# A two-layer hybrid network on one core: places and number of buffers for split weights, products per bank, and the plan of the modulation blocks

## The chip, the cores and the metric

The kernel runs on one core of a Trainium2 chip. The metric is the time of one execution on the device in microseconds (us), the median of several runs. Five engines work side by side: TensorE (PE: matmuls, PEld: its weight loads), VectorE (DVE), ScalarE (ACT), GpSimd (POOL) and SyncE (SP), which here issues most of the DMAs. In the rows, "L114" is line 114 of the kernel, and times are counted from the start of the span.

## The reference, cut to what matters

One sequence of 256 tokens with 1024 features goes through two layers of three sub-layers each: an FFN, a mixer, an FFN. The mixer of the first layer is a hybrid of a gated linear recurrence and a state-space part, that of the second an mLSTM. Before each sub-layer the input is normalised and modulated by a shift and a scale, behind it a gate is applied; shift, scale and gate come from a vector `c` through a large matrix `ada_w`.

```python
c_act = jax.nn.silu(c)
for layer in range(DEPTH):
    mod = (c_act @ ada_w[layer] + ada_b[layer]).reshape(bsz, N_SUB, 3, D_MODEL)[:, :, :, None, :]

    def modulate(t, sub):
        return rms_norm(t, norm_g[layer, sub]) * (1.0 + mod[:, sub, 1]) + mod[:, sub, 0]

    h = modulate(x, 0)
    x = x + HALF_STEP * (1.0 + mod[:, 0, 2]) * swiglu(h, ffn_w_gate[layer, 0], ffn_w_up[layer, 0], ffn_w_down[layer, 0])
    h = modulate(x, 1)
    if layer % 2 == 0:
        y = hybrid_mixer(h, ...)
    else:
        y = mlstm_block(h, ...)
    x = x + (1.0 + mod[:, 1, 2]) * y.astype(x.dtype)
    h = modulate(x, 2)
    x = x + HALF_STEP * (1.0 + mod[:, 2, 2]) * swiglu(h, ffn_w_gate[layer, 1], ffn_w_up[layer, 1], ffn_w_down[layer, 1])
return rms_norm(x, final_norm_g)

def swiglu(h, w_gate, w_up, w_down):
    return (jax.nn.silu(h @ w_gate) * (h @ w_up)) @ w_down
```

All of it is in float32; the FFN's inner width is 2816, that is 22 blocks of 128.

## The kernel before, in words

**Layout.** Activations are kept transposed, features on the partitions and the 256 tokens along the free dimension: `x` is eight tiles of 128 x 256. The six sub-layers s = 0 to 5 are FFN, hybrid, FFN, FFN, mLSTM, FFN; "the third FFN" is s = 3.

**Weights.** All weights are one stream of 2928 tiles of 128 x 128, in the order of use, cut into 366 pieces of eight tiles (128 x 1024 float32, 512 KB each). `Weights._piece` (L97) loads a piece into a raw buffer (L101, on SP's queue; pool `rawp`, three buffers), ACT rounds it to a high part `whi` (L113), and VectorE subtracts that from the raw piece and leaves the low part `wlo` (L114). Both parts live in pool `partp`, with six buffers of each. Pieces are made four ahead of use (`LEAD`). So the DMA of a piece waits for the split of the piece that had its raw buffer before, and a cast waits for a pair of parts that TensorE is done with.

**Products.** An activation is split in the same manner into a high and a low part that stand side by side (`hb` for the normalised input, `ph`, `yb`, `ysb`, `ylb` for the inputs of output projections; the split is L339 on ACT and L340 on VectorE). A product with a weight tile is the sum of three matmuls: high weight by high and by low activation, and low weight by high activation (`multiply`, L346 to L348, 256 columns each). The output projections of the FFNs and of the mLSTM make the first two with one matmul of 512 columns (L451) over both parts, into the two halves of a bank, and the third with one of 256 (L453) into the first half; VectorE then adds both halves to `x`, in two instructions (L458). The last column group of the last FFN and the hybrid's projection have three products of 256 columns.

**Places.** `PLACES` gives each piece the place of its two parts modulo 512 bytes in a partition, by an offset in a buffer that is 128 elements longer than a piece. The parts of projections stand at 448 and at 0 or 256 in turn; the second FFN's gate/up takes four sorts in turn; elsewhere two sorts in turn, with (128, 0) at every eleventh piece.

**FFN.** `ffn` (L473) starts with four banks of the first blocks on an input that isn't normalised yet (`begin`, L380, with L393 to L395), while VectorE computes the norm and then eight chunks of the normalised input: L360 on VectorE, L362 on ACT for the high part, L363 on VectorE for the low part. Then gate/up runs block by block: 16 tiles into one bank, Silu on ACT (L481), the product on VectorE (`fg`, L482), and its split (`ph`, L339 and L340). The output projection (`out_project`, L411) goes over eight column groups, each with 22 products, one for each `ph`.

**Modulation.** `ADA_PLAN` spreads the 144 blocks of `ada_w` over the pieces: for each entry a sub-layer, a range of pieces counted from its start, and the blocks. `ada_block` (L225) loads 512 KB (L230, SP's queue) and multiplies and sums on VectorE (L232). A block is issued behind the newest split. Blocks 72 to 95 are the modulation of s = 3, 96 to 119 that of s = 4. In the third FFN VectorE also prepares the mLSTM's gate weights (`mlstm_weights`, L824, with DMAs on POOL's queue).

The order of the instructions on each engine is made when the kernel is built, by a scheduler that follows priorities in program order, the dependencies, and what `behind` and `issue_after` demand.

## Time and profile before

| | us |
|---|---|
| time, median of 3 runs | 1138.89 (1138.03 to 1142.32) |
| the profiled execution, its own time | 1137.13 |
| its span | 1135.4 |
| TensorE busy | 1109.3 (98%) |
| TensorE's weight loads busy | 1057.5 (93%) |
| VectorE busy | 955.4 (84%) |
| ScalarE busy | 642.0 (57%) |
| mean granted clock of TensorE | 0.995 |
| read from HBM | 269.77 MB, mean 239 GB/s |

Busy time of an engine is the time in which at least one of its instructions was running. Matmuls are pipelined, so a matmul's own duration is longer than the step from one to the next; the step is what counts on TensorE. In rows of the timeline the bracket gives the idle time ahead of an instruction and what ended it. In the chain of waits the program is followed back from its last instruction, at each step to what released it. The profile's page cuts the span into 40 equal slices of 28.4 us; a digit is tenths.

### The profile page before, as it was taken

To read this page: it belongs to the slowest core of one execution; us is meant where nothing else is said; L and a number is where in the kernel's file an instruction comes from. 1 tells how busy PE (TensorE), PEld (TensorE's weight loads), DVE (VectorE), ACT (ScalarE), POOL (GpSimd) and SP (SyncE) were. 2 spreads that over 40 slices of the span, in tenths; PEclk is the share of its full clock that TensorE was granted. 3 is DMA by queue.
4 is the path that set the end of the run, shared out by engine and by line. 5 is a ranking of instruction groups with operands and counts; after the bars stand their busy time and mean duration, and the time that the engine had idled before them with its cause. 6 is when DMAs were issued, how large, how long until landed. Compare 5 with 4: busy or idle time off the path is not lost.

```text
span 1135.4 us, 21905 instructions
## 1 busy us (share of the span) xinstructions
PE 1109.3 (98%) x8548; PEld 1057.5 (93%) x8548; DVE 955.4 (84%) x1831; ACT 642.0 (57%) x1074; POOL 8.8 (1%) x25
## 2 busy tenths in 40 slices
PE   7999999999999999999999997999999999999997
PEld 6999988999989999998899997889999889999987
DVE  7999999999889798889889888889879988766562
ACT  4464545888976564444554444447765556554542
POOL 0000000000000000000000000010000000000000
PEclk9999999999999999999999998999999999999999
DMA  8989999555555558888849889972532374775551
GB/s 318 357 304 350 383 330 326 207 192 194 186 174 178 201 200 324 311 306 317 291 157 324 309 318 328 328 275 94 168 112 93 113 235 156 269 241 194 188 201 39
DMA packets 75273, 272.25 MB, mean 240 GB/s; under 512 B 8449, under 2 KB 9121, under 8 KB 75170
## 3 DMA queue, kind: packets, MB, share of 16 engines
q1 hardware_dynamic: 74160, 268.99, 67.4%
q8 instruction: 67, 1.10, 0.4%
q0 software_dynamic: 432, 1.10, 0.4%
q10 hardware_dynamic: 578, 0.76, 0.2%
q14 instruction: 36, 0.29, 0.1%
HBM read 269.77 MB, written 1.05 MB: 239 GB/s over the span
## 4 chain that ended last, share of the span: by engine, by line
PE 61%; DVE 18%; DMA 13%; ACT 5%; issue 3%; ACTq 0%; SPq 0%; DVEq 0%
PE od L451 12%; DMA wraw<-in_wst_dram 11%; DVE wlo L114 7%; PE gu L346 7%; PE gu L347 7%; PE gu L348 7%; PE od L453 6%; DVE ada L232 3%; ACT whi L113 3%; DVE hb L363 1%; DMA wgr<-in_ml_wg_dram 1%; DVE ht L360 1%; PE od L346 1%; PE up L347 1%; PE up L348 1%
## 5 line engine op out<-in xcount | busy, mean ns | idle before, releaser
L113 ACT CAST whi<-wraw 128x1024 fp32r<-128x1024 f32 x364 | 380.0, 1048 | 281.6 <-DMA wraw<-in_wst_dram 172.9
L114 DVE TENSOR_TENSOR wlo<-wraw,whi 128x1024 fp32r<-128x1024 f32 x366 | 446.1, 1221 | 97.1 <-ACT whi L113 95.1
L347 PE MATMUL gu<-hb,whi 128*128 128x256 f32 x1312 | 362.7, 278 | 0.1
L348 PE MATMUL gu<-hb,wlo 128*128 128x256 f32 x1312 | 362.4, 277 | 0.0
L346 PE MATMUL gu<-hb,whi 128*128 128x256 f32 x1312 | 359.1, 278 | 1.6 <-ACT hb L362 1.5
L347 PEld LDWEIGHTS gu<-hb,whi 128*128 128x128 f32 x1312 | 247.5, 189 | 0.3 <-DVE hb L363 0.3
L348 PEld LDWEIGHTS gu<-hb,wlo 128*128 128x128 f32 x1312 | 247.5, 189 | 0.0
L346 PEld LDWEIGHTS gu<-hb,whi 128*128 128x128 f32 x1312 | 245.2, 189 | 2.1 <-ACT hb L362 2.0
L451 PE MATMUL od<-ph,whi 128*128 128x512 f32 x682 | 236.2, 394 | 5.8 <-DVE ph L340 5.8
L453 PE MATMUL od<-ph,wlo 128*128 128x256 f32 x682 | 190.0, 279 | 0.0
L232 DVE SCALAR_TENSOR_TENSOR ada<-ada,cact 128x1024 f32<-128x1024 f32 x144 | 174.9, 1217 | 0.2 <-DMA ada<-in_adaT_dram 0.2
L451 PEld LDWEIGHTS od<-ph,whi 128*128 128x128 f32 x682 | 129.5, 190 | 33.7 <-DVE ph L340 6.6
L453 PEld LDWEIGHTS od<-ph,wlo 128*128 128x128 f32 x682 | 129.6, 190 | 0.0
L339 ACT CAST ph<-fg 128x256 fp32r<-128x256 f32 x88 | 35.2, 406 | 98.1 <-DVE fg L482 97.8
L458 DVE SCALAR_TENSOR_TENSOR x<-od,gate,x 128x256 f32<-128x256 f32 x87 | 41.5, 480 | 20.1 <-PE od L348 9.7
L340 DVE TENSOR_TENSOR ph<-fg,ph 128x256 fp32r<-128x256 f32 x88 | 36.6, 420 | 12.9 <-ACT ph L339 12.9
L451 PE MATMUL od<-yb,whi 128*128 128x512 f32 x128 | 44.2, 392 | 0.0
L346 PE MATMUL zz<-hb,whi 128*128 128x256 f32 x128 | 37.2, 290 | 0.0
L348 PE MATMUL zz<-hb,wlo 128*128 128x256 f32 x128 | 36.9, 288 | 0.0
L347 PE MATMUL zz<-hb,whi 128*128 128x256 f32 x128 | 36.7, 287 | 0.0
L453 PE MATMUL od<-yb,wlo 128*128 128x256 f32 x128 | 35.5, 279 | 0.0
L362 ACT ACTIVATE hb<-ht,shift 128x256 fp32r<-128x256 f32 x48 | 22.6, 505 | 22.9 <-DVE ht L360 22.9
(407 smaller groups left out, 1896.1 us busy)
## 6 DMA issues: line engine op xcount, KB each, us to landing
wraw<-in_wst_dram SPq DMA_DIRECT2D x366, 512.0 KB, 4.4
ada<-in_adaT_dram SPq DMA_DIRECT2D x144, 512.0 KB, 5.3
xn<-in_x_dram SPq DMA_DIRECT2D x2, 512.0 KB, 4.1
wgr<-in_ml_wg_dram POOLq DMA_DIRECT2D x3, 256.0 KB, 5.2
out_dram<-res ACTq DMA_DIRECT2D x2, 128.0 KB, 2.3
out_dram<-res SPq DMA_DIRECT2D x2, 128.0 KB, 2.1
out_dram<-res SPq DMA_DIRECT2D x1, 256.0 KB, 2.5
out_dram<-res ACTq DMA_DIRECT2D x1, 256.0 KB, 2.6
```

The lines of the kernel that those rows point to most:

```text
L113: raw_hi = nc.scalar.copy(hi, raw)
L114: self.last = nc.vector.tensor_tensor(out=lo, in0=raw, in1=hi.bitcast(F32), op=ALU.subtract)
L232: nc.vector.scalar_tensor_tensor(out=raw, in0=raw, scalar=1.0, in1=cact, op0=ALU.mult, op1=ALU.mult, accum_out=mods[s][:, m:m + 1])
L339: nc.scalar.copy(hi, src)
L340: nc.vector.tensor_tensor(out=both[:, 1, :], in0=src, in1=hi.bitcast(F32), op=ALU.subtract)
L346: m = nc.tensor.matmul(dst, wh, both[:, 0, :], start=start, stop=False, skip_group_check=True)
L347: nc.tensor.matmul(dst, wh, both[:, 1, :], start=False, stop=False, skip_group_check=True)
L348: nc.tensor.matmul(dst, wl, both[:, 0, :], start=False, stop=stop, skip_group_check=True)
L362: hi = nc.scalar.activation(h[k][:, 0, :], t, AF.Identity, bias=sh[:, k:k + 1])
L451: nc.tensor.matmul(bank, wh, both.rearrange("p i t -> p (i t)"), start=(k == 0), stop=False, skip_group_check=True)
L453: nc.tensor.matmul(sums[0], wl, both[:, 0, :], start=False, stop=(k == len(rhs) - 1), skip_group_check=True)
L458: nc.vector.scalar_tensor_tensor(out=xs_t[d], in0=part, scalar=g[:, d:d + 1], in1=xs_t[d], op0=ALU.mult, op1=ALU.add)
```

## The change

The parts of a piece get places by tag, in place of offsets: three tags a, b and c in turn (piece number modulo 3) with two buffers each, laid out with pads so that high and low part stand at (448, 320), (64, 448) and (448, 64) modulo 512. There are still six of each, now without the 128 spare elements. The raw ring has four buffers. The eight blocks 96 to 103 move from the plan of the third FFN to that of the second. All output projections use `project`, three matmuls of 256 columns into one half of a bank, and one addition to `x` per column group.

```diff
-PLACES = []
...
-    if _w:
-        PLACES.append((128, 192) if _w[0] in (1, 8) else (448, 256 * (_i % 2)))
-    elif _s == 2:
-        PLACES.append(((448, 320), (64, 448), (448, 64), (320, 192))[_i % 4])
-    else:
-        PLACES.append((128, 0) if _n % 11 == 6 else (448, 64 + 256 * (_i % 2)))
+PLACES = (("wloa", 320), ("whia", 448), ("whic", 448), ("wlob", 448), ("whib", 64), ("wloc", 64))
+FIRST_PLACE = 64
...
-    (2, (6, 60), range(64, 96)), (3, (6, 60), range(96, 136)), (5, (6, 40), range(136, 144)),
+    (2, (6, 60), range(64, 104)), (3, (6, 60), range(104, 136)), (5, (6, 40), range(136, 144)),
...
-        oh, ol = ((n - 64) % 512 // 4 for n in PLACES[i])
-        hi = self.part_pool.tile([P, w + 128], F32R, tag="whi", name=f"whi{i}")[:, oh:oh + w]
-        lo = self.part_pool.tile([P, w + 128], F32R, tag="wlo", name=f"wlo{i}")[:, ol:ol + w]
+        hi, lo = (self.part_pool.tile([P, w], F32R, tag=f"{n}{'abc'[i % 3]}", name=f"{n}{i}") for n in ("whi", "wlo"))
...
-    rawp = ctx.enter_context(tc.tile_pool(name="rawp", bufs=3))
-    partp = ctx.enter_context(tc.tile_pool(name="partp", bufs=6))
+    rawp = ctx.enter_context(tc.tile_pool(name="rawp", bufs=4))
+    partp = ctx.enter_context(tc.tile_pool(name="partp", bufs=2))
+    at = FIRST_PLACE
+    for tag, place in PLACES:
+        if (place - at) % 512:
+            partp.tile([P, (place - at) % 512 // 4], F32, name=f"pad_{tag}", bufs=1)
+        partp.tile([P, PIECE * P], F32R, tag=tag, name=f"place_{tag}")
+        at = place
...
-                sums = [dst]
-            elif s == 5 and d == ND - 1:
-
-                sums = [mm_bank(f"od{s}_{d}")[:, 0:T]]
-                project(sums[0], rhs)
             else:
-
-
-                bank = mm_bank(f"od{s}_{d}")
-                sums = [bank[:, 0:T], bank[:, T:2 * T]]
-                for k, both in enumerate(rhs):
-                    wh, wl = W.next()
-                    nc.tensor.matmul(bank, wh, both.rearrange("p i t -> p (i t)"), start=(k == 0), stop=False,
-                                     skip_group_check=True)
-                    nc.tensor.matmul(sums[0], wl, both[:, 0, :], start=False, stop=(k == len(rhs) - 1),
-                                     skip_group_check=True)
+                dst = mm_bank(f"od{s}_{d}")[:, 0:T]
+                project(dst, rhs)
...
-            for part in sums[::-1]:
-                nc.vector.scalar_tensor_tensor(out=xs_t[d], in0=part, scalar=g[:, d:d + 1], in1=xs_t[d],
-                                               op0=ALU.mult, op1=ALU.add)
+            nc.vector.scalar_tensor_tensor(out=xs_t[d], in0=dst, scalar=g[:, d:d + 1], in1=xs_t[d],
+                                           op0=ALU.mult, op1=ALU.add)
```

The changed kernel is shorter, so its line numbers are lower: L457 is what L482 was, L329 what L340 was, L97 what L114 was, L221 what L232 was, L433 what L458 was, L349, L352 and L395 what L360, L363 and L406 were, and L335 to L337 what L346 to L348 were. On TensorE 810 matmuls come in, on VectorE 39 instructions go.

The first place is VectorE at the end of the third FFN's gate/up, before: `ph3_20` and `ph3_21` are the last two split blocks, `wlo` the low parts of pieces, `ada` modulation blocks.

```order
L482 TENSOR_TENSOR fg3_20_8784<-fg3_20_8784,gu3_20_8720 128x256
L232 SCALAR_TENSOR_TENSOR ada124_8830,mod5_8653<-ada124_8830,cact_107 128x1024
L340 TENSOR_TENSOR ph3_20_8787<-fg3_20_8784,ph3_20_8787 128x256
L114 TENSOR_TENSOR wlo234_8868<-wraw234_8865,whi234_8867 128x1024
L114 TENSOR_TENSOR wlo235_8890<-wraw235_8887,whi235_8889 128x1024
L482 TENSOR_TENSOR fg3_21_8857<-fg3_21_8857,gu3_21_8790 128x256
L232 SCALAR_TENSOR_TENSOR ada125_8893,mod5_8653<-ada125_8893,cact_107 128x1024
L340 TENSOR_TENSOR ph3_21_8860<-fg3_21_8857,ph3_21_8860 128x256
```

The same place after:

```order
L457 TENSOR_TENSOR fg3_20_9138<-fg3_20_9138,gu3_20_9074 128x256
L221 SCALAR_TENSOR_TENSOR ada126_9181,mod5_8827<-ada126_9181,cact_116 128x1024
L329 TENSOR_TENSOR ph3_20_9141<-fg3_20_9138,ph3_20_9141 128x256
L97 TENSOR_TENSOR wlo234_9219<-wraw234_9216,whi234_9218 128x1024
L221 SCALAR_TENSOR_TENSOR ada127_9222,mod5_8827<-ada127_9222,cact_116 128x1024
L97 TENSOR_TENSOR wlo235_9252<-wraw235_9249,whi235_9251 128x1024
L457 TENSOR_TENSOR fg3_21_9208<-fg3_21_9208,gu3_21_9144 128x256
L329 TENSOR_TENSOR ph3_21_9211<-fg3_21_9208,ph3_21_9211 128x256
```

Two modulation blocks stand between `fg3_20` and `ph3_21` in both, but the second has moved ahead of `wlo235` and doesn't stand directly ahead of `ph3_21` any more. They are `ada126` and `ada127` where `ada124` and `ada125` stood; since the plan starts at block 104 and not at 96, 24 blocks of it are ahead of `ph3_21`, where 30 were.

The second place is VectorE at the end of the second FFN's gate/up, before:

```order
L114 TENSOR_TENSOR wlo168_6612<-wraw168_6609,whi168_6611 128x1024
L232 SCALAR_TENSOR_TENSOR ada87_6615,mod3_5727<-ada87_6615,cact_107 128x1024
L370 CAST hb_96<-shift3_6683 128x8x2
L259 TENSOR_TENSOR scale3_6684<-mod3_5727,cols_95 128x8
L371 TENSOR_TENSOR hb_96<-shift3_6683,hb_96 128x8x2
L260 SCALAR_TENSOR_TENSOR scale3_6684<-scale3_6684,cols_95 128x8
L114 TENSOR_TENSOR wlo169_6637<-wraw169_6634,whi169_6636 128x1024
L482 TENSOR_TENSOR fg2_21_6601<-fg2_21_6601,gu2_21_6537 128x256
L340 TENSOR_TENSOR ph2_21_6604<-fg2_21_6601,ph2_21_6604 128x256
```

And after:

```order
L97 TENSOR_TENSOR wlo168_6807<-wraw168_6804,whi168_6806 128x1024
L97 TENSOR_TENSOR wlo169_6837<-wraw169_6834,whi169_6836 128x1024
L457 TENSOR_TENSOR fg2_21_6796<-fg2_21_6796,gu2_21_6729 128x256
L221 SCALAR_TENSOR_TENSOR ada93_6840,mod3_5807<-ada93_6840,cact_116 128x1024
L329 TENSOR_TENSOR ph2_21_6799<-fg2_21_6796,ph2_21_6799 128x256
```

Here the last block of modulation ahead of `ph2_21` is `ada93`, where it was `ada87`, so 30 blocks of this plan are ahead of it, where 24 were; the shift and scale of the next sub-layer (`shift3`, `scale3`), which stood between, come earlier in the program.

The third place is VectorE and TensorE at the start of the third FFN, while the chunks of the normalised input are made (`ht3_k` is chunk k before its shift, `hb` the normalised input's parts; `gu3_f0` to `gu3_f3` are the four first banks, `gu3_2` and `gu3_3` the next blocks). VectorE before:

```order
L406 TENSOR_TENSOR fg3_0_7382<-gu3_f0_7226,rs3_7201 128x256
L363 SCALAR_TENSOR_TENSOR hb_96<-ht3_4_7366,shift3_6683,hb_96 128x256
L363 SCALAR_TENSOR_TENSOR hb_96<-ht3_5_7370,shift3_6683,hb_96 128x256
L360 SCALAR_TENSOR_TENSOR ht3_6_7374<-x_94,scale3_6684,rs3_7201 128x256
L360 SCALAR_TENSOR_TENSOR ht3_7_7378<-x_94,scale3_6684,rs3_7201 128x256
L114 TENSOR_TENSOR wlo193_7323<-wraw193_7320,whi193_7322 128x1024
L363 SCALAR_TENSOR_TENSOR hb_96<-ht3_6_7374,shift3_6683,hb_96 128x256
L363 SCALAR_TENSOR_TENSOR hb_96<-ht3_7_7378,shift3_6683,hb_96 128x256
L408 COPY shc_g3_0_7384<-gu3_f0_7226 128x1
L406 TENSOR_TENSOR fu3_0_7386<-gu3_f1_7227,rs3_7201 128x256
```

VectorE after:

```order
L97 TENSOR_TENSOR wlo194_7782<-wraw194_7779,whi194_7781 128x1024
L352 SCALAR_TENSOR_TENSOR hb_105<-ht3_4_7736,shift3_6899,hb_105 128x256
L352 SCALAR_TENSOR_TENSOR hb_105<-ht3_5_7740,shift3_6899,hb_105 128x256
L349 SCALAR_TENSOR_TENSOR ht3_6_7744<-x_103,scale3_6900,rs3_7571 128x256
L97 TENSOR_TENSOR wlo193_7693<-wraw193_7690,whi193_7692 128x1024
L352 SCALAR_TENSOR_TENSOR hb_105<-ht3_6_7744,shift3_6899,hb_105 128x256
L349 SCALAR_TENSOR_TENSOR ht3_7_7748<-x_103,scale3_6900,rs3_7571 128x256
L395 TENSOR_TENSOR fu3_0_7756<-gu3_f1_7597,rs3_7571 128x256
L397 COPY shc_u3_0_7758<-gu3_f1_7597 128x1
L395 TENSOR_TENSOR fg3_1_7760<-gu3_f2_7598,rs3_7571 128x256
L352 SCALAR_TENSOR_TENSOR hb_105<-ht3_7_7748,shift3_6899,hb_105 128x256
```

A split (`wlo194`), the products `fu3_0` and `fg3_1` and two copies now stand ahead of the last low part of `hb`. TensorE, at the products of block 2 with the last chunk (the last rows of `whi190` here), before:

```order
L347 MATMUL gu3_2_7408<-hb_96,whi190_7232 128x256
L348 MATMUL gu3_2_7408<-hb_96,wlo190_7233 128x256
L346 MATMUL gu3_2_7408<-hb_96,whi190_7232 128x256
L347 MATMUL gu3_2_7408<-hb_96,whi190_7232 128x256
L348 MATMUL gu3_2_7408<-hb_96,wlo190_7233 128x256
L346 MATMUL gu3_2_7408<-hb_96,whi191_7262 128x256
```

And after:

```order
L336 MATMUL gu3_3_7845<-hb_105,whi192_7662 128x256
L337 MATMUL gu3_3_7845<-hb_105,wlo192_7663 128x256
L335 MATMUL gu3_2_7778<-hb_105,whi190_7602 128x256
L335 MATMUL gu3_3_7845<-hb_105,whi192_7662 128x256
L336 MATMUL gu3_3_7845<-hb_105,whi192_7662 128x256
L337 MATMUL gu3_3_7845<-hb_105,wlo192_7663 128x256
L335 MATMUL gu3_3_7845<-hb_105,whi192_7662 128x256
L336 MATMUL gu3_3_7845<-hb_105,whi192_7662 128x256
L336 MATMUL gu3_2_7778<-hb_105,whi190_7602 128x256
L337 MATMUL gu3_2_7778<-hb_105,wlo190_7603 128x256
L335 MATMUL gu3_2_7778<-hb_105,whi191_7632 128x256
```

In the order after, matmuls of block 3 (`gu3_3`) stand between those of block 2; eleven of them are ahead of the row that reads the last chunk's low part (the second L336 of `gu3_2`).

## Rows read from the trace of the kernel before

**Rows 1.** The page: busy time of each engine over the span (us, share, instructions), and the granted clock of TensorE in 40 slices.

```profile
PE 1109.3 (98%) x8548; PEld 1057.5 (93%) x8548; DVE 955.4 (84%) x1831; ACT 642.0 (57%) x1074; POOL 8.8 (1%) x25
...
PEclk9999999999999999999999998999999999999999
```

**Rows 2.** The page: the chain of waits that ended last, share of the span by engine.

```profile
PE 61%; DVE 18%; DMA 13%; ACT 5%; issue 3%; ACTq 0%; SPq 0%; DVEq 0%
```

**Rows 3.** Busy time by stage: start and end of each stretch in us, its length, each engine's busy us and its instructions, TensorE's granted clock, share of the DMA engines, GB/s. The stretches are the first FFN's gate/up from 60 us on, the second FFN's gate/up and output projection, the third's gate/up and output projection.

```profile
60.00:139.00 79.00, 79.00 (x696) 79.00 (x696) 73.41 (x120) 42.47 (x68) 0.00 (x0) 1.00 0.95 351
...
402.30:512.00 109.70, 109.54 (x962) 109.12 (x961) 92.38 (x143) 58.03 (x87) 0.00 (x0) 1.00 0.82 294
512.00:572.40 60.40, 60.40 (x359) 53.51 (x358) 51.64 (x82) 30.61 (x41) 1.06 (x2) 1.00 0.87 296
584.80:694.10 109.30, 109.30 (x962) 109.30 (x961) 95.69 (x159) 52.31 (x79) 1.08 (x2) 1.00 0.85 300
694.10:764.30 70.20, 64.44 (x358) 56.20 (x357) 60.02 (x91) 33.17 (x47) 2.67 (x7) 0.93 0.87 313
```

**Rows 4.** TensorE's timeline in the third FFN's output projection: start in us, duration in us, engine, line, operation, tiles, shapes, and in brackets the idle time before it and what ended it.

```profile
700.66 0.39 PE L451 MATMUL od<-ph,whi 128*128 128x512 f32 x1
700.88 0.28 PE L453 MATMUL od<-ph,wlo 128*128 128x256 f32 x1
703.82 0.79 PE L451 MATMUL od<-ph,whi 128*128 128x512 f32 x1 [2.66 <-DVE ph L340]
...
707.93 0.79 PE L451 MATMUL od<-ph,whi 128*128 128x512 f32 x1 [3.10 <-DVE ph L340]
...
708.73 0.63 PE L451 MATMUL od<-ph,whi 128*128 128x512 f32 x1
...
709.37 0.63 PE L451 MATMUL od<-ph,whi 128*128 128x512 f32 x1
...
713.85 0.48 PE L451 MATMUL od<-ph,whi 128*128 128x512 f32 x1
```

**Rows 5.** VectorE's timeline in the same stretch.

```profile
703.35 0.42 DVE L340 TENSOR_TENSOR ph<-fg,ph 128x256 fp32r<-128x256 f32 x1
703.70 2.36 DVE L114 TENSOR_TENSOR wlo<-wraw,whi 128x1024 fp32r<-128x1024 f32 x2
...
706.31 1.22 DVE L232 SCALAR_TENSOR_TENSOR ada<-ada,cact 128x1024 f32<-128x1024 f32 x1
...
707.46 0.42 DVE L340 TENSOR_TENSOR ph<-fg,ph 128x256 fp32r<-128x256 f32 x1
```

**Rows 6.** Waits in the third FFN's gate/up, 584.8 to 694.1 us: who waited for what, us in total, times, longest us.

```profile
ACT whi L113 <- DMA wraw<-in_wst_dram: 26.3, 19, 3.1
```

**Rows 7.** Waits of SP's queue over the whole span, same columns.

```profile
SPq L101 <- DVE wlo L114: 554.8, 243, 16.5
```

**Rows 8.** The page: DMA issues, with count, KB each and median us from issue to landing.

```profile
wraw<-in_wst_dram SPq DMA_DIRECT2D x366, 512.0 KB, 4.4
```

**Rows 9.** VectorE's timeline: the split of the last `ph` of the first FFN and of the second.

```profile
142.69 0.42 DVE L340 TENSOR_TENSOR ph<-fg,ph 128x256 fp32r<-128x256 f32 x1
...
518.53 0.43 DVE L340 TENSOR_TENSOR ph<-fg,ph 128x256 fp32r<-128x256 f32 x1 [0.47 <-ACT ph L339]
```

**Rows 10.** TensorE's timeline at the ends of stretches without a wait: two wide pairs of the first FFN's projection, three pieces of the hybrid's projection, three pieces of the second FFN's gate/up, one piece of the third's.

```profile
149.89 0.39 PE L451 MATMUL od<-ph,whi 128*128 128x512 f32 x1
...
150.23 0.39 PE L451 MATMUL od<-ph,whi 128*128 128x512 f32 x1
...
352.90 0.28 PE L346 MATMUL od<-ysb,whi 128*128 128x256 f32 x1
...
361.46 0.28 PE L346 MATMUL od<-ysb,whi 128*128 128x256 f32 x1
...
452.20 0.28 PE L346 MATMUL gu<-hb,whi 128*128 128x256 f32 x1
...
460.36 0.28 PE L346 MATMUL gu<-hb,whi 128*128 128x256 f32 x1
...
620.35 0.28 PE L346 MATMUL gu<-hb,whi 128*128 128x256 f32 x1
...
623.18 0.28 PE L346 MATMUL gu<-hb,whi 128*128 128x256 f32 x1
```

**Rows 11.** The timeline of ACT, then of TensorE, in the hybrid's output projection.

```profile
368.12 1.05 ACT L113 CAST whi<-wraw 128x1024 fp32r<-128x1024 f32 x1 [1.06 <-DMA wraw<-in_wst_dram]
...
366.81 0.38 PE L346 MATMUL od<-ylb,whi 128*128 128x256 f32 x1 [0.55 <-ACT ylb L339]
...
369.53 0.51 PE L346 MATMUL od<-ylb,whi 128*128 128x256 f32 x2 [0.72 <-ACT ylb L339]
```

**Rows 12.** VectorE's timeline at the start of the third FFN.

```profile
585.12 1.22 DVE L114 TENSOR_TENSOR wlo<-wraw,whi 128x1024 fp32r<-128x1024 f32 x1
586.26 0.87 DVE L363 SCALAR_TENSOR_TENSOR hb<-ht,shift,hb 128x256 fp32r<-128x256 f32 x2
...
587.12 0.41 DVE L406 TENSOR_TENSOR fu<-gu_f,rs 128x256 f32<-128x256 f32 x1
587.45 0.14 DVE L408 COPY shc_u<-gu_f 128x1 f32<-128x1 f32 x1
```

**Rows 13.** The page: the group of the additions to `x` behind output projections: count, busy us, mean ns of one, idle time before and its releaser.

```profile
L458 DVE SCALAR_TENSOR_TENSOR x<-od,gate,x 128x256 f32<-128x256 f32 x87 | 41.5, 480 | 20.1 <-PE od L348 9.7
```

9 lines of the change are left out of this document (removed).

## Prediction, made before the change was run

> **What bounds the kernel now.** I began with the page's busy row and the row of granted clock: TensorE is busy for 1109.3 of 1135.4 us, VectorE for 955.4, and one of the 40 slices, the 26th, has a lower clock [rows 1]. The chain's groups come next: TensorE has 61% of the chain, but VectorE has 18% and DMA 13%, so in places the weights' supply ends last [rows 2]. To find the place I cut the span by stage [rows 3]. The FFNs' gate/up stretches are full of matmuls: 109.54 of 109.70 us in the second FFN, 109.30 of 109.30 in the third. The output projections differ: 60.40 us in the second FFN, all busy at clock 1.00; 70.20 us in the third, with 64.44 busy at 0.93. Same instructions, 9.8 us more. The timeline of TensorE in that stretch shows why [rows 4]: after 700.88 it waits 2.66 us, after one more pair 3.10 us, both for `ph` of L340 on VectorE, and then runs at the lower of its two levels (1.2 GHz): pairs every 0.64 us (708.73, 709.37) until about 713.85, where the same pair takes 0.34 in a warm stretch [rows 10]. From 700.66 to 713.85 there are 11 pairs: 13.19 us against 11 x 0.34 = 3.74, so the stall costs 9.45 us.
>
> VectorE's rows say what was late [rows 5]. Gate/up ended at 694.10, yet block 20's `ph` starts at 703.35 and block 21's at 707.46, and ahead of each stands a split (L114) and a modulation block (L232). VectorE wasn't full: 95.69 of 109.30 us busy, 13.6 us idle [rows 3], while ACT's casts waited 26.3 us in this stretch for a raw piece to land [rows 6]. The issue of a raw piece in turn waits for the split three pieces earlier, 554.8 us over the run on SP's queue [rows 7], and a transfer takes 4.4 us at the median [rows 8], against the 2.72 us in which TensorE uses one up (452.20 to 460.36 is three pieces) [rows 10]. So third-FFN VectorE falls behind for two reasons together: it has 40 modulation blocks, and a late piece can't be made good, since the raw ring is only three deep.
>
> **The change part by part.** The sum is made against the profiled execution, 1137.1 us (span 1135.4); it is 1.8 us under the median of 1138.9.
>
> *Modulation moved, with the fourth raw buffer: -9.4 us.* The last `ph` is the 22nd factor of the projection's first column group, so TensorE comes to it 21 pairs after 694.10, at 694.10 + 21 x 0.34 = 701.2; it ended at 707.46 + 0.42 = 707.9, which is 6.7 us late [rows 5]. By the two orders, 30 modulation blocks (96 to 125) stand ahead of it before and 24 (104 to 127) after. Each takes VectorE 1.15 us from its start to the start of the next instruction (706.31 to 707.46) [rows 5], so six fewer give 6.9 us: alone this would just do. The fourth buffer adds one piece, 2.72 us, of lead to each transfer, and fewer DMAs of 512 KB compete there, so the 26.3 us of late pieces shrink too. I take all 9.45 us; bounds 0 (stall as before) and -9.8 (both projections equal).
>
> Those six stand ahead of the second FFN's last `ph` now, 6.9 us, and all eight cost VectorE 9.2 there. It is busy 92.38 of 109.70 us in gate/up: 17.3 us of cover, and 8.8 more in the projection [rows 3]. But the slack at the end is small now: the last `ph` ends at 518.53 + 0.43 = 518.96 [rows 9], and TensorE comes to it at 512.0 + 21 x 0.34 = 519.1. So the second FFN is on time only if its idle time, which is waiting for late pieces, really shrinks. For that speaks the first FFN: with 24 blocks on 26 pieces, a higher rate than 40 on 54, its last `ph` ends at 143.11 [rows 9] where 139.0 + 7.14 = 146.1 would do, and TensorE stays full with three buffers, at 351 GB/s [rows 3]. The second FFN of the change wants 54 weight pieces and 40 blocks, 94 x 0.524 MB, in 54 x 2.72 = 147 us: 335 GB/s, below this. I take 0; bounds 0 and +9.4 (the stall moves here whole).
>
> *Three products in one bank: 0.* Per tile two matmuls (512 and 256 columns) become three of 256. The wide pair goes 149.89 to 150.23, 0.340 us; three narrow ones take (460.36 - 452.20)/72 = 0.1133 each, 0.340 together [rows 10]. 810 tiles change (682 + 128), and the columns are the same 768. The step from two bank halves to one drops 39 evacuations (L458) of 0.480 us, 18.7 us of VectorE [rows 13]; nearly all lie beside matmuls, so I count 0 on the path. Bounds: -2 (a few stand ahead of the next norm) and, where the slow step below holds, +13.6.
> The Trainium skill ("TensorE: Matmul & The Clock Gate", section "Back-to-back issue gap") gives the isolated gap of a warm matmul as N/2.4 + 2.5 ns, so that a third matmul pays the fixed part once more: 810 x 2.5 ns = an estimate of 2.0 us slower. The rows above show 0.340 us both ways, so here the trace doesn't agree; by the page the time would come out at 1128.
>
> *Places: -4.0 us.* Before, the sort (128, 0), at every eleventh narrow piece outside the second FFN, is slow: such a piece runs from 620.35 to 623.18, 2.83 us in place of 2.72 [rows 10]. There are 20 of them: 20 x 0.11 = 2.2 us. In the hybrid's projection the step is 118.9 ns: 352.90 to 361.46 is three pieces, 8.56/72 [rows 10]. The second FFN's gate/up, where sorts already take turns, runs at 113.3 (452.20 to 460.36); the change uses three of its four sorts everywhere, so I expect 113.3 elsewhere too. The hybrid's projection has 16 pieces; two fall on the waits below, and 14 x 24 x 5.6 ns = 1.9 us, of which I take 1.8; bounds -6 (all stretches above 113.3) and the slow step's cost as a rival below.
>
> *Fourth raw buffer elsewhere: -1.3 us.* In the hybrid's projection ACT waits 1.06 us for a raw piece, and its `ylb` cast, queued behind that whi cast, holds TensorE 0.55 and 0.72 us [rows 11]; 2.72 us more of lead covers both. Bounds 0 and -2.5 (the same again in slower matmuls behind the waits).
>
> *The other side: norms, +1.7 us.* The change's VectorE order at the start of the third FFN has a split (wlo194) and two L395 (the old L406) ahead of the last chunk's low part which before came behind it. Their steps are 1.14 (585.12 to 586.26) and 0.33 (587.12 to 587.45): 1.14 + 2 x 0.33 = 1.8 us [rows 12]. TensorE's order has eleven matmuls moved ahead of the first that reads this chunk: 11 x 0.113 = 1.25. Before, no wait and no spare is shown; so I take 0.55 us of waiting, in the last three sub-layers, whose orders are alike: 1.7. Bounds 0 and +5.4 (each loses the 1.8).
>
> SP and POOL issue the same DMAs in the same number; only the eight move, each behind an earlier split. The splits read and write as many bytes as before. 0 for both.
>
> Sum: -9.4 - 4.0 - 1.3 + 1.7 = -13.0, so 1124.1 in a profiled run; 1.8 more for the median: **1126 us**.
>
> **The rivals.** *The stall moves to the second FFN.* Then 9.4 us come back: 1126 + 9.4 = 1135. For it: a slack of 0.1 us against 6.9 us more work ahead; the second FFN then carries what the third did before, but for the third's preparation of mLSTM gate weights. Against it: 17.3 us idle, the fourth buffer, the first FFN's rows. 0.15.
> *Stall stays in the third FFN*, if six blocks fewer don't do and the fourth buffer gives no lead (because the next DMA still queues behind other transfers), also about 1135. Against it: 6.9 us freed for 6.7 late. 0.06.
> *The slow step holds (slower).* 118.9 against 113.3 ns is 16.8 ns a tile. It shows in a projection with three products, the hybrid's, and there it lasts for three pieces in a row; the wide pairs don't have it [rows 10]. If three products in the 810 changed tiles run at it: +13.6 us, 1140, no gain left; it decides from 13.0/0.0168 = 774 tiles. Gate/up has 352 tiles in each of four FFNs; with half of these 1408 too, 11.8 us more: 1151, the price I give this rival. Against it: 72 matmuls in a row at 113.3 with these sorts. 0.08.
>
> **How the numbers follow.** Forecast 0.64, rivals 0.15, 0.06, 0.08; 0.07 is left for effects I name no price for, on both sides. A measurement tells 0.5% from no change, 5.7 us: faster is below 1133.2, slower above 1144.6. Faster: 0.64 and 0.08 of the unnamed and partial stalls, 0.72; same: the two stalls less that part, 0.19; slower 0.09. The forecast's own range is 1121 (places -6, norms 0, the rest as taken: 1126 - 2.0 - 1.7 = 1122, and 1 less for `ylb`) to 1131 (norms +5.4, `ylb` 0); the range that holds the time in 8 of 10 takes 2 us more below, for evacuations ahead of a norm, and reaches to the stalls above: 1119 to 1137.
>
> **What would show it.** Right: the third FFN's projection takes 60 us at clock 1.00, with no wait for `ph`; the second's stays at 60; L433 has 48 rows in place of the 87 of L458; ACT's waits for raw pieces shrink in the third FFN from 26.3 us. The step of pieces is 2.72 us all over, and no piece at 2.83. At the three norms a wait of about 0.55 us for `hb`. Wrong: waits for `ph` in the second FFN, or rows of 0.119 us in the projections.

## The result, and the profile after

The changed kernel takes 1127.45 us (median of 4 runs, 1126.65 to 1128.43) against 1138.46 for the kernel before; the ratio is 0.990, with an interval of 0.987 to 0.993. It is 11.0 us faster, where 12.9 were forecast (1126). The profiled execution took 1128.43 us, the slowest of the four, with a span of 1126.7; its differences against the profiled execution before are 8.7 us in all.

The page after shows the busy times, the chain by engine (one line), and the group of the additions to `x`; they answer to [rows 1, 2, 13]:

```profile
PE 1106.6 (98%) x9358; PEld 1085.6 (96%) x9358; DVE 939.1 (83%) x1792; ACT 641.2 (57%) x1074; POOL 8.7 (1%) x25
...
PE 86%; DVE 7%; ACT 3%; DMA 2%; issue 1%; ACTq 0%; DVEq 0%; SPq 0%
...
L433 DVE SCALAR_TENSOR_TENSOR x<-od,gate,x 128x256 f32<-128x256 f32 x48 | 23.1, 481 | 30.4 <-PE od L337 30.4
```

In the chain TensorE's share went from 61% to 86%, VectorE's from 18% to 7%, DMA's from 13% to 2%: the supply of weights hardly ends last anywhere now. Busy time says nothing of this: TensorE had 98% before and has 98% after. The chain is no proof of a gain, though. The kernel before with three products per tile and nothing else (below) is 12.7 us slower than before, and its chain looks nearly like the one after:

```profile
PE 84%; DVE 8%; ACT 3%; DMA 2%; issue 1%; ACTq 0%; SPq 0%
```

With slower matmuls TensorE ends last more often too. What was gained has to be read by stage.

By stage, with the same columns as [rows 3] (second FFN's gate/up and output projection, third's gate/up and projection, and the hybrid as a whole):

```profile
403.90:513.88 109.98, 109.86 (x963) 109.50 (x963) 101.66 (x163) 57.99 (x88) 0.00 (x0) 1.00 0.89 325
513.88:574.09 60.21, 60.21 (x535) 60.21 (x533) 47.78 (x69) 29.47 (x39) 1.06 (x2) 1.00 0.88 308
586.40:696.09 109.69, 109.58 (x963) 109.24 (x963) 97.98 (x163) 55.17 (x85) 1.07 (x2) 1.00 0.87 306
696.09:756.29 60.20, 60.20 (x534) 60.20 (x533) 45.96 (x66) 29.26 (x39) 2.69 (x7) 1.00 0.83 282
...
198.09:388.12 190.03, 184.34 (x1496) 174.42 (x1496) 166.83 (x369) 145.72 (x283) 0.00 (x0) 0.98 0.54 184
```

The third FFN's projection went from 70.20 us at clock 0.93 to 60.20 at 1.00. The second FFN's is what it was, though VectorE is busy for 101.66 us in its gate/up (92.38 before). From the first matmul of each sub-layer to the next one's, the two traces differ by -0.6 us in the first FFN, +2.9 in the hybrid (187.1 to 190.0), 0.0 in the second FFN, -9.8 in the third, -0.6 in the mLSTM and 0.0 in the last FFN; another 0.6 lies ahead of the first weights. In this pair of traces the gain of the whole is that of one stage, and the hybrid gave a part back.

How far can the length of a stage in one trace be trusted? Two kernels of the experiments have, in the hybrid, the same instructions in the same order on TensorE, VectorE and ACT as one of this pair. The first row is the changed kernel with the old plan, to be held against the 190.03 us above; the second is the kernel before with the new plan, against 187.12 us before.

```profile
198.90:385.43 186.53, 180.76 (x1497) 171.25 (x1497) 166.59 (x369) 145.58 (x283) 0.00 (x0) 1.00 0.57 187
198.84:388.16 189.32, 183.94 (x1496) 175.71 (x1496) 168.65 (x374) 146.76 (x284) 0.00 (x0) 0.99 0.58 187
```

So the hybrid differs by 2 to 4 us between executions with one and the same order. The trace after has the lower clock in two places of it (0.86 in the mean from 210 to 222 us, 0.96 from 340 us on); the first of these rows has it nowhere. The 2.9 us are therefore a number of this trace and not the price of the change.

The last `ph` of the second and of the third FFN on VectorE, as in [rows 5, 9]:

```profile
517.72 0.42 DVE L329 TENSOR_TENSOR ph<-fg,ph 128x256 fp32r<-128x256 f32 x1
...
699.34 0.42 DVE L329 TENSOR_TENSOR ph<-fg,ph 128x256 fp32r<-128x256 f32 x1 [0.47 <-ACT ph L328]
```

Gate/up ends at 513.88 and 696.09, so 21 products further TensorE wants them at 521.0 and 703.2: both come some 3 us early, where the third was 6.7 us late.

Over the whole run, ACT's casts wait less for raw pieces; before, that group had 172.9 us on the page:

```profile
ACT whi L96 <- DMA wraw<-in_wst_dram: 53.6, 49, 3.4
```

In the third FFN's gate/up this wait of 26.3 us [rows 6] has gone from the list, and what casts wait longest for there is TensorE, that is a free pair of parts: at these eight casts the splits are as far ahead as six pairs allow.

```profile
ACT whi L96 <- PE gu L336: 10.6, 8, 1.7
```

### The profile page after: what moved, and what is told of

The parts are those of the page before. It is cut to its first block, busy times and chain, and to the rows that moved or that the text cites. A ratio compares the mean times of both kernels' runs of the same rounds, so it can differ in the third digit from the quotient of the medians.

```text
span 1126.7 us, 23501 instructions
## 1 busy us (share of the span) xinstructions
PE 1106.6 (98%) x9358; PEld 1085.6 (96%) x9358; DVE 939.1 (83%) x1792; ACT 641.2 (57%) x1074; POOL 8.7 (1%) x25
## 4 chain that ended last, share of the span: by engine, by line
PE 86%; DVE 7%; ACT 3%; DMA 2%; issue 1%; ACTq 0%; DVEq 0%; SPq 0%
PE gu L336 13%; PE gu L335 13%; PE gu L337 13%; PE od L335 9%; PE od L336 9%; PE od L337 9%; DVE wlo L97 2%; DMA wraw<-in_wst_dram 1%; PE zz L337 1%; PE zz L335 1%; PE zz L336 1%; ACT whi L96 1%; PE up L336 1%; PE up L337 1%; PE up L335 1%
## 5 line engine op out<-in xcount | busy, mean ns | idle before, releaser
L97 DVE TENSOR_TENSOR wlo<-wraw,whi 128x1024 fp32r<-128x1024 f32 x366 | 445.9, 1221 | 86.1 <-ACT whi L96 84.4
L336 PE MATMUL gu<-hb,whi 128*128 128x256 f32 x1312 | 362.1, 277 | 0.2
L337 PE MATMUL gu<-hb,wlo 128*128 128x256 f32 x1312 | 361.3, 277 | 0.0
L335 PE MATMUL gu<-hb,whi 128*128 128x256 f32 x1312 | 358.3, 278 | 1.6 <-ACT hb L351 1.5
L336 PEld LDWEIGHTS gu<-hb,whi 128*128 128x128 f32 x1312 | 247.4, 189 | 0.7 <-DVE hb L352 0.6
L335 PEld LDWEIGHTS gu<-hb,whi 128*128 128x128 f32 x1312 | 244.8, 189 | 2.5 <-ACT hb L351 2.0
L337 PEld LDWEIGHTS gu<-hb,wlo 128*128 128x128 f32 x1312 | 247.2, 189 | 0.0
L336 PE MATMUL od<-ph,whi 128*128 128x256 f32 x704 | 194.3, 276 | 0.0
L337 PE MATMUL od<-ph,wlo 128*128 128x256 f32 x704 | 194.3, 276 | 0.0
L335 PE MATMUL od<-ph,whi 128*128 128x256 f32 x704 | 194.3, 276 | 0.0
L221 DVE SCALAR_TENSOR_TENSOR ada<-ada,cact 128x1024 f32<-128x1024 f32 x144 | 174.9, 1218 | 0.0
L336 PEld LDWEIGHTS od<-ph,whi 128*128 128x128 f32 x704 | 132.2, 188 | 0.0
L335 PEld LDWEIGHTS od<-ph,whi 128*128 128x128 f32 x704 | 132.2, 188 | 0.0
L337 PEld LDWEIGHTS od<-ph,wlo 128*128 128x128 f32 x704 | 132.2, 188 | 0.0
L433 DVE SCALAR_TENSOR_TENSOR x<-od,gate,x 128x256 f32<-128x256 f32 x48 | 23.1, 481 | 30.4 <-PE od L337 30.4
L329 DVE TENSOR_TENSOR ph<-fg,ph 128x256 fp32r<-128x256 f32 x88 | 36.5, 420 | 13.3 <-ACT ph L328 13.3
L318 ACT ACTIVATE sq_o<-x 128x256 f32<-128x256 f32 x42 | 17.5, 418 | 49.4 <-DVE x L433 49.1
L456 ACT ACTIVATE fg<-gu 128x256 f32<-128x256 f32 x82 | 30.7, 377 | 13.5 <-PE gu L337 13.4
L335 PE MATMUL zz<-hb,whi 128*128 128x256 f32 x128 | 37.0, 289 | 0.0
L337 PE MATMUL zz<-hb,wlo 128*128 128x256 f32 x128 | 36.9, 288 | 0.0
```

The source lines that it names most:

```text
L97: self.last = nc.vector.tensor_tensor(out=lo, in0=raw, in1=hi.bitcast(F32), op=ALU.subtract)
L221: nc.vector.scalar_tensor_tensor(out=raw, in0=raw, scalar=1.0, in1=cact, op0=ALU.mult, op1=ALU.mult, accum_out=mods[s][:, m:m + 1])
L318: square = nc.scalar.activation(q, x, AF.Square).ins
L329: nc.vector.tensor_tensor(out=both[:, 1, :], in0=src, in1=hi.bitcast(F32), op=ALU.subtract)
L335: m = nc.tensor.matmul(dst, wh, both[:, 0, :], start=start, stop=False, skip_group_check=True)
L336: nc.tensor.matmul(dst, wh, both[:, 1, :], start=False, stop=False, skip_group_check=True)
```

## The experiments

Each kernel was timed against the kernel before on the same chip, whose median was 1137.5 to 1137.8 us in these rounds. Ten kernels were run.

### Plan or buffer: four kernels

The kernel before with the plan alone:

```diff
-    (2, (6, 60), range(64, 96)), (3, (6, 60), range(96, 136)), (5, (6, 40), range(136, 144)),
+    (2, (6, 60), range(64, 104)), (3, (6, 60), range(104, 136)), (5, (6, 40), range(136, 144)),
```

> The kernel before with the eight modulation blocks moved and nothing else (three raw buffers, old places, wide projections). Theory of the prediction: six blocks fewer ahead of the third FFN's last ph give 6.9 us where 6.7 us were missing, so the plan alone just cures the stall there: third projection 60 to 61 us in place of 70.2, time about 1138.5 - 9.4 = 1129. Its weak point is the second FFN: with a slack of 0.1 us and 6.9 us more work ahead of its last ph, three buffers deep. Rival, the fourth buffer is what cures: with three buffers the stall moves to the second FFN (its projection 65 to 70 us) or stays, time 1135 to 1139.

Measured: 1134.23 us (10 runs from 1128.12 to 1142.06), ratio 0.998 (0.995 to 1.000). In the profiled execution, 1130.92 us, the third projection took 61.83 us:

```profile
696.07:757.90 61.83, 61.01 (x358) 53.63 (x357) 52.77 (x79) 30.93 (x43) 2.58 (x7) 1.00 0.84 292
```

One wait was left there, of 0.82 us for `ph`, and the second FFN stayed at 60.3. So in this execution six blocks fewer do just about cure the stall, as reckoned. But it lies 3.3 us under the median: the executions of this kernel spread over 14 us, where the four of the changed kernel lie within 1.8, and the median lies between the two expectations, 3.3 us below the kernel before, with an interval that reaches to no gain. That the stall is cured in every execution is not shown.

The changed kernel with the old plan:

```diff
-    (2, (6, 60), range(64, 104)), (3, (6, 60), range(104, 136)), (5, (6, 40), range(136, 144)),
+    (2, (6, 60), range(64, 96)), (3, (6, 60), range(96, 136)), (5, (6, 40), range(136, 144)),
```

> The changed kernel with the old plan of modulation blocks (40 of them in the third FFN), four raw buffers. Theory of the prediction (blocks and buffer add up): the fourth buffer gives each transfer 2.72 us more lead, but 30 blocks are ahead of the third FFN's last ph again, so part of the stall is back: third projection 62 to 67 us, time 1129 to 1134 (1127.5 in the changed kernel). Rival, the fourth buffer alone cures: third projection 60 us, time 1127.5 within 1.5.

Measured: 1127.43 us, ratio 0.991 (0.989 to 0.992). The third projection:

```profile
693.46:753.65 60.19, 60.19 (x534) 60.19 (x533) 47.94 (x70) 29.47 (x39) 2.63 (x7) 1.00 0.87 303
```

The rival holds: with four buffers 30 blocks ahead of the last `ph` do no harm, and the moved blocks are worth nothing (1127.43 against 1127.45).

The changed kernel with three buffers, with the new and with the old plan:

```diff
-    rawp = ctx.enter_context(tc.tile_pool(name="rawp", bufs=4))
+    rawp = ctx.enter_context(tc.tile_pool(name="rawp", bufs=3))
```

> The changed kernel with three raw buffers in place of four, the rest as changed. If the buffer is needed for the second FFN, its projection takes 65 to 70 us and the time is 1132 to 1137; if the plan alone does it for both FFNs, both projections take 60 us and the time is 1127.5 within 1.5. On the hybrid, which is 3 us slower in the changed kernel (waits for the normalised input near its start): if the fourth buffer's transfers in flight are the cause it goes back to about 163 us in all, if not it stays at 166.

> The changed kernel with three raw buffers and the old plan: of the change only places and three products per tile are left. Theory of the prediction: the stall of the third FFN is back whole, 69 to 70 us for its projection, time 1127.5 + 9.4 = 1137; places give their 3.7 us still, so it is not above the kernel before. Rival, the 39 evacuations fewer or the new order on VectorE cure the stall: 60 to 62 us there and a time of 1127.5 to 1129.

Measured: 1136.30 us (ratio 0.998, 0.996 to 1.000) and 1143.97 us (1.005, 1.003 to 1.007). The stages of the first are the third projection and the hybrid:

```profile
704.20:764.40 60.20, 60.20 (x534) 60.20 (x533) 49.01 (x72) 30.41 (x41) 2.58 (x7) 1.00 0.86 299
198.68:395.49 196.81, 184.49 (x1497) 176.10 (x1496) 170.98 (x375) 147.05 (x284) 0.00 (x0) 0.97 0.57 184
```

and of the second, in the same order:

```profile
701.09:769.20 68.11, 63.16 (x534) 62.27 (x533) 57.19 (x84) 33.42 (x46) 2.63 (x7) 0.95 0.92 319
200.64:392.65 192.01, 182.96 (x1497) 174.52 (x1496) 169.42 (x375) 146.73 (x284) 0.00 (x0) 0.98 0.56 184
```

Without the buffer and with the old plan the stall is back, so the 39 additions fewer don't cure it. But the time of that kernel is 6.4 us above the kernel before, where I had expected it not to be above at all: at three buffers places and three products together cost time, and 4.9 us of it lie in the hybrid of these traces (187.12 to 192.01). With the new plan the stall is gone in both FFNs at three buffers, against my doubt of the second. But the three-buffer kernel loses elsewhere: its hybrid is 6.8 us longer than the changed kernel's in these two traces (the expectation's 163 and 166 us are the steps of its weight matmuls alone, 187 and 190 as a whole). The kernel with the old plan has the same order there, but for one modulation block at the start, and takes 192.01 us; so 4.8 of these 6.8 us can be a difference between executions. What follows is that the hybrid doesn't get shorter when the fourth buffer is taken away. At the start of the hybrid a cast on ACT waits 3.27 us for its piece; the split behind it on VectorE waits for the cast, and behind that split stands the addition to `x` (L433) of the last column group, whose squares TensorE needs. ACT's row, then VectorE's, then TensorE's, of the kernel with three buffers and the new plan:

```profile
200.88 1.04 ACT L96 CAST whi<-wraw 128x1024 fp32r<-128x1024 f32 x1 [3.27 <-DMA wraw<-in_wst_dram]
...
201.96 1.23 DVE L97 TENSOR_TENSOR wlo<-wraw,whi 128x1024 fp32r<-128x1024 f32 x1 [0.73 <-ACT whi L96]
203.10 0.48 DVE L433 SCALAR_TENSOR_TENSOR x<-od,gate,x 128x256 f32<-128x256 f32 x1
...
204.14 1.02 PE L287 MATMUL rst_n<-ones,sq_o 128*128 128x1 f32 x4 [4.13 <-ACT sq_o L318]
```

| third FFN's projection / time, us | three raw buffers | four raw buffers |
|---|---|---|
| old plan | 68.11 / 1143.97 | 60.19 / 1127.43 |
| new plan | 60.20 / 1136.30 | 60.20 / 1127.45 |

Together: with three buffers the plan is worth 1143.97 - 1136.30 = 7.7 us (3.3 in the kernel before); with four, nothing. The buffer is worth 16.5 us with the old plan and 8.9 with the new one. Casts wait 178.5 and 183.8 us for raw pieces in the three-buffer kernels (old plan, new plan), 62.2 and 53.6 with four. The two remedies for the third FFN are alternatives, not a sum.

The kernel before with a fourth buffer and nothing else is missing, and it can't be had: twelve part buffers that are 512 bytes per partition longer than a piece take 6 KB, a raw buffer takes 4 KB, and beside the old layout the pools of the mLSTM would lack 2.2 KB. The new layout needs pads of 0.5 KB, so it frees 5.5. What the places do for this kernel is first of all to make room for the buffer.

### Products and places: three kernels

The changed kernel with wide products in the projections:

```diff
-                dst = mm_bank(f"od{s}_{d}")[:, 0:T]
-                project(dst, rhs)
+                bank = mm_bank(f"od{s}_{d}")
+                sums = [bank[:, 0:T], bank[:, T:2 * T]]
...
+                    nc.tensor.matmul(bank, wh, both.rearrange("p i t -> p (i t)"), start=(k == 0), stop=False,
+                                     skip_group_check=True)
+                    nc.tensor.matmul(sums[0], wl, both[:, 0, :], start=False, stop=(k == len(rhs) - 1),
+                                     skip_group_check=True)
...
```

> The changed kernel with the old wide products in the output projections (one matmul of 512 and one of 256 columns per tile, two additions to x per column group), the rest as changed. Theory of the prediction: 0.340 us a tile both ways, so the FFN projections stay at 60.2 us and the time at 1127.5 within 1.5. By the page's gap rule the third matmul costs 2.5 ns a tile, 2.0 us in 810 tiles, so this kernel would take 1125.5. Rival, VectorE's 39 additions fewer matter: 1129 to 1132.

The kernel before with this edit the other way, and nothing else:

> The kernel before with three products of 256 columns and one addition in all output projections, old places (448 with 0 or 256 in the projections), three raw buffers, old plan. Theory of the prediction: no cost on TensorE, 1137.5 within 2. Rival, the slow step of 118.9 ns belongs to three products at these old places: 16.8 ns in up to 810 tiles, 5 to 13.6 us more, and the FFN projections take 61 to 63 us where no stall is.

The kernel before with the new places alone (the three tags and the pads of the diff above):

> The kernel before with the new places alone (three tags with two buffers), wide products, three raw buffers, old plan. Theory of the prediction: slow pieces of the sort (128, 0) and the 118.9 ns steps go, 3.7 us as the two traces show it, time 1133.5. Rival: the tags also let the scheduler put casts of later pieces ahead of the norm, and with three raw buffers the hybrid's start waits longer for the pieces; what the steps give goes there: 1137 to 1142, with a hybrid of 190 to 193 us in all (187.1 before).

Measured: 1134.35 us (ratio 0.996, 0.994 to 0.998), 1150.36 us (1.010, 1.006 to 1.014) and 1145.00 us (1.006, 1.004 to 1.008). Neither half of this pair is free alone. The first lies above all three of its expected times; the second comes out as its rival said; the third lies 3 us above its rival's range. In the wide kernel three pieces of the second FFN's projection, 541.07 to 549.44, take 2.79 us each:

```profile
541.07 0.39 PE L437 MATMUL od<-ph,whi 128*128 128x512 f32 x1
...
549.44 0.39 PE L437 MATMUL od<-ph,whi 128*128 128x512 f32 x1
```

In the kernel with three products at the old places, it is 2.83 in the projection, and the step stays slow in the next FFN's gate/up, 2.85:

```profile
544.28 0.28 PE L346 MATMUL od<-ph,whi 128*128 128x256 f32 x1
...
552.76 0.28 PE L346 MATMUL od<-ph,whi 128*128 128x256 f32 x1
...
602.85 0.28 PE L346 MATMUL gu<-hb,whi 128*128 128x256 f32 x1
...
611.41 0.28 PE L346 MATMUL gu<-hb,whi 128*128 128x256 f32 x1
```

The same gate/up pieces (194 to 196, same places, same three products) go at 2.72 in the kernel before, where a wide projection ran ahead of them:

```profile
595.86 0.28 PE L346 MATMUL gu<-hb,whi 128*128 128x256 f32 x1
...
604.02 0.28 PE L346 MATMUL gu<-hb,whi 128*128 128x256 f32 x1
```

And in the changed kernel, three products at the new places, again 2.72:

```profile
541.08 0.28 PE L335 MATMUL od<-ph,whi 128*128 128x256 f32 x1
...
549.24 0.28 PE L335 MATMUL od<-ph,whi 128*128 128x256 f32 x1
```

The slow step in the gate/up of the kernel with three products ends all at once: the piece that starts at 628.53, the second of the sort (128, 0) there, still takes 2.85, and the next 2.72, as do those behind it of the sorts that were slow before:

```profile
628.53 0.28 PE L346 MATMUL gu<-hb,whi 128*128 128x256 f32 x1
...
631.38 0.28 PE L346 MATMUL gu<-hb,whi 128*128 128x256 f32 x1
...
634.10 0.28 PE L346 MATMUL gu<-hb,whi 128*128 128x256 f32 x1
```

A projection of an FFN without a stall so takes 60.31 us (old places, wide), 62.52 (old places, three products), 61.75 (new places, wide) or 60.20 (new places, three products). As to the step of the matmuls, the two edits belong together. As to the time at three buffers and with the old plan, all three kernels are slower than before, by 12.7 us (three products alone), 7.3 (places alone) and 6.4 (both). The rival of the slow step, +13.6 us for 810 tiles, is real, but only at the old places: the kernel with three products alone is 12.7 us slower than before, though its third projection, at 66.41 us, stalls less. The page's rule of the gap (the Trainium skill, "TensorE: Matmul & The Clock Gate", section "Back-to-back issue gap"), by which two matmuls would beat three by an estimate of 2.0 us, fits at neither set of places: at the new ones wide is 6.9 us slower than three products, 1.55 of it in each full FFN projection, and at the old ones it is 12.7 us faster.

The kernel with the places alone has a hybrid of 191.6 us (187.1 before) and the stall in the third FFN still (67.93 us), the hybrid as its rival said; its wide projections are at 61.75 us where no stall is, 1.4 us each above the kernel before, and neither expectation had that.

### The hybrid's start: two kernels, and one for `ylb`

Where does the changed kernel's hybrid lose time in the trace after? TensorE's timeline, at 213.54, shows a wait for the high part of a chunk of the normalised input, and then the lower of the two levels, a step of 0.21 us in place of 0.113 up to about 218:

```profile
213.54 0.28 PE L337 MATMUL xbc<-hb,wlo 128*128 128x256 f32 x1
214.92 0.71 PE L335 MATMUL xbc<-hb,whi 128*128 128x256 f32 x2 [1.10 <-ACT hb L351]
...
216.71 0.41 PE L336 MATMUL xbc<-hb,whi 128*128 128x256 f32 x1
216.92 0.41 PE L337 MATMUL xbc<-hb,wlo 128*128 128x256 f32 x1
```

ACT's timeline after says why the chunk is late: casts of pieces that TensorE needs much later stand ahead of the chunks (L351), and wait for their pieces to land, 1.59 and 0.67 us.

```profile
209.37 1.05 ACT L96 CAST whi<-wraw 128x1024 fp32r<-128x1024 f32 x1 [1.59 <-DMA wraw<-in_wst_dram]
210.33 0.51 ACT L351 ACTIVATE hb<-ht,shift 128x256 fp32r<-128x256 f32 x1
...
213.41 1.05 ACT L96 CAST whi<-wraw 128x1024 fp32r<-128x1024 f32 x1 [0.67 <-DMA wraw<-in_wst_dram]
214.37 0.50 ACT L351 ACTIVATE hb<-ht,shift 128x256 fp32r<-128x256 f32 x1
```

By the orders these are the casts of pieces 74 and 75, ahead of chunks 3 and 6; the kernel before has pieces 71 to 73 ahead of chunk 3, and 74 only ahead of the last chunk. The changed kernel with the old plan has the same order, but there the pieces landed earlier (the second of these casts waits 0.22 us), TensorE's wait is 0.3 us, and the clock stays up: the order is a risk that not every execution pays for. The test is to hold pieces 73 to 75 back:

```diff
         if late:
             W.behind(i0 + 6, 1, chain[6][0])
+            for n in (7, 8, 9):
+                W.behind(i0 + n, 0, chain[7][1])
+                W.behind(i0 + n, 1, chain[7][0])
```

> The changed kernel; at the hybrid's start the casts and splits of its pieces 7, 8 and 9 are placed behind the last chunk of the normalised input on ACT and VectorE (nothing else is changed). If TensorE's waits at 212 to 218 us there come from casts that wait for a raw piece ahead of the chunks in ACT's order, they go with the half clock behind them: hybrid 186 in place of 190.0 us, time 1123 to 1125. Rival, the chunks are late on their own chain (VectorE to ACT and back): hybrid 189 to 190, time 1127.

Measured: 1124.16 us (6 runs from 1123.47 to 1126.56), ratio 0.987 (0.984 to 0.990); the hybrid takes 183.87 us, and the step between 213 and 221 us is 0.113. It beats both kernels, by 13.5 us and, by the two medians, by 3.3; its hybrid is also 2.7 us below the 186.53 us of the kernel with the old plan, where the late pieces cost little.

The same with three buffers:

> The kernel with the norm's chunks first, and three raw buffers in place of four. If the fourth buffer's worth in the hybrid is only that casts wait for pieces ahead of the chunks, it is worth nothing once the chunks are first: 1124 to 1126. If it is also the first wait there (the squares of the last column group, queued behind a cast that waits for its piece, 4.3 us with three buffers): start of the hybrid 3 to 5 us longer, time 1128 to 1132.

Measured: 1132.22 us, ratio 0.995 (0.993 to 0.997), hybrid 187.54 us. It is 4.1 us better than three buffers without this edit, and 8.1 behind four buffers with it, so the second expectation holds in its time. But the long wait for the squares isn't in this trace; the loss is spread, 3.7 us in the hybrid, against 183.87, and 1.2 to 1.5 in each of the first three FFNs. What the buffer saves is thus not one wait but some of many.

Last, the `ylb` section, where the forecast's 1.3 us didn't come. TensorE's waits in the changed kernel, to be held against [rows 11]:

```profile
366.88 0.38 PE L335 MATMUL od<-ylb,whi 128*128 128x256 f32 x1 [0.26 <-ACT ylb L328]
368.25 0.39 PE L336 MATMUL od<-ylb,whi 128*128 128x256 f32 x1 [0.98 <-DVE ylb L329]
```

They are as long as before in sum (1.24 against 1.27), but the second ends with VectorE's low part, and ACT's casts of `ylb` wait for `lru_x` on VectorE. I took a modulation block out of its way, on top of the edit above:

```diff
-    (0, (17, 43), range(16, 40)), (0, (43, 65), range(48, 64)), (1, (26, 45), range(40, 48)),
+    (0, (17, 43), range(16, 40)), (0, (43, 65), range(48, 64)), (1, (26, 38), range(40, 48)),
```

> The kernel with the chunks of the norm first in the hybrid, and the hybrid's eight modulation blocks (40 to 47) spread over its pieces 26 to 38 in place of 26 to 45, so that the last doesn't stand on VectorE among the products for ylb. In the changed kernel TensorE loses some 2.7 us in the ylb section to lru_x and ylb on VectorE, with one modulation block of 1.2 us shortly ahead. If that block is in the way: hybrid's projection 1 to 2 us shorter than with the norm alone, time 1122 to 1123.5. If not (splits of weights stand between the products all the same): 1124 within 1.

Measured: 1127.93 us (5 runs from 1125.78 to 1128.72), ratio 0.990 (0.989 to 0.992), 3.8 us slower than with the norm alone and outside both expectations. The waits of the `ylb` section went, but the part of the hybrid ahead of the projection grew from 138.09 to 142.44 us, with a stretch of lower clock in it (0.96 from 260 to 300 us, where the kernel with the norm alone has 1.00):

```profile
260.00:300.00 40.00, 38.26 (x313) 37.29 (x312) 37.74 (x70) 35.01 (x69) 0.00 (x0) 0.96 0.72 235
```

and these waits of TensorE ahead of the projection:

```profile
PE ri L335 <- ACT xlb L328: 1.4, 1, 1.4
PE rst_g L287 <- ACT sq_g L318: 1.0, 1, 1.0
```

In these two traces the denser plan costs more ahead of the projection than the block cost at `ylb`. As a hybrid differs by 2 to 4 us between executions of one order, only the medians bear on the whole, and that the plan makes these two waits is not shown.

## Why the prediction was right, point by point

*The stall, -9.4 us*: the third FFN lost 9.8 us. The mechanism (late pieces, no lead, `ph` late, then the lower clock) stands, and the rival that it moves to the second FFN fell: its `ph` came 3 us early with 101.66 us of VectorE. The step "alone this would just do" holds of the plan in one execution (61.83 us), but its other half was undersized: in the changed kernel the buffer by itself is worth the whole, and the plan adds nothing to it. I treated it as one piece more of lead for a lateness of 6.7 us; by the waits of casts, 172.9 to 53.6 us in the whole run, it does far more than that.

*Three products, 0*: right of the change (60.31 to 60.20 us), wrong as a sentence on its own. The price of three products depends on the places, and I priced the two edits apart: by the runs +12.7 us for the one, +7.3 us for the other, both in three-buffer kernels.

*Places, -4.0 us*: by the steps nearly right. The steps of more than 114 and up to 130 ns behind matmuls with weights exceed 114 ns by 9.5 us in all before and by 6.2 after, that is -3.3. The slow pieces at every eleventh place are gone. But "2.72 us all over" failed: near its start the second FFN's gate/up now has 24 matmuls in a row that take 2.85 us.

```profile
410.36 0.28 PE L335 MATMUL gu<-hb,whi 128*128 128x256 f32 x1
...
413.21 0.28 PE L336 MATMUL gu<-hb,whi 128*128 128x256 f32 x1
```

As a gain of time the new places show at three buffers only where three products run already (1150.36 to 1143.97 us); against the kernel before they cost 7.3 us alone and 6.4 together with three products. What they gave instead, the room for the buffer, the prediction doesn't name.

*Fourth buffer elsewhere, -1.3 us*: failed. The waits for `ylb` stayed, with VectorE in the place of the DMA; the wait removed had another right behind it.

*Norms, +1.7 us*: right in place, too large. At each of the three starts one step is about 0.27 us too long, 0.8 in all: from 588.68 to 589.18 in the third FFN is one, two matmuls in 0.50 us. A start loses a little more by slow steps as those just shown: from its first matmul to the end of gate/up the third FFN takes 122.0 us after and 121.75 before, though its four pieces of 2.83 us are gone.

*Missed*: the start of the hybrid. I read the orders at the third FFN's start and not at the hybrid's, where the same holds: the scheduler put casts ahead of the chunks that the path needs. With three buffers and the new places the order has no piece beyond 72 ahead of chunk 3, with four it has 73 and 74, so it is the fourth buffer that lets them go there; the remedy is to hold them back and not to take the buffer away. By the medians of the kernels with and without the chunks first this order costs 3.3 us.

Sum by stage: -9.8 - 0.6 - 0.6 - 0.6 + 2.9 = -8.7 in the profiled pair, and -11.0 between medians; the execution of the trace after lies 1.0 us above its median, with the two falls of the clock in its hybrid.

That the sum came out within 1.5 us is in part luck. Taken in the order of the runs, places and products cost 6.4 us (1137.54 to 1143.97), the buffer gives 16.5 (to 1127.43), and the plan 0.0. The forecast had places, products and norms at -4.0 + 0 + 1.7 = -2.3, and plan and buffer at -9.4 - 1.3 = -10.7. Two errors, 8.7 us one way and 5.8 the other, cancel for the most part. Since the edits don't add up, another order of them would share out the gain in another way.

## What to carry to other kernels

When a stream of weights goes through a ring, look first at which queue has to finish what before the next transfer may start: one more raw buffer can be worth more than all the balancing of the engine that empties the ring, and a layout that makes room for it can be worth more than what it does to the matmuls. When an edit makes places or product forms different, time them in all combinations before a verdict on one, since a form may be free at one place and cost nearly 4% of a stretch at another. After any edit that lets a scheduler run further ahead, read the order at every stage's start: an instruction that waits for a transfer must not stand ahead of one that the path needs. And before a difference of a few us in one stage is explained, look at a second trace with the same order there.

## What the runs showed of the hardware that was not expected

Which form of the product is faster depended on how the weights lie: 0.1133 us a matmul of 256 columns for three products at the new places, 0.1178 at the old places of the projections, 0.340 a wide pair at the old places and 0.349 at the new ones. The kernels differ in the place modulo 512 bytes, but with it in tags, pads and the length of the buffers, so that it is this remainder and nothing else in the layout is not shown. Nor do place and form settle the step: gate/up pieces whose places and products were the same took 2.72 us behind a wide projection and 2.85 behind one of three products, and this lasted until 631.38, behind a piece of another sort. What in the memory or the array makes it so, no run here shows.

The same instructions in the same order on three engines took 190.03 us in one execution, with two falls of the granted clock, and 186.53 in another without any.
